# Scale and shift of the second adaLN branch: summed over the partitions by GpSimd instead of TensorE, with the conditioning loads moved forward

## The chip, the cores and the metric

One Trainium2 chip, one of its cores. The metric is the device time of one launch in microseconds (us). The kernel before took 1150.16 us, the median of three runs (1148.13 to 1151.42).

## The reference

One decoder block on x of 1024 tokens by 1024 channels, float32. A conditioning vector c gives six vectors of 1024 numbers: shift, scale and gate for a mixer and for an MLP. The mixer normalises x, projects it, runs a pooling and a state-space mixer, and projects back ("output projection", `w_out`). The MLP normalises again, applies scale_f and shift_f, and runs two large matrix products.

```
mod = silu(c) @ w_ada + b_ada                       # 1024 -> 6 * 1024
shift_m, scale_m, gate_m, shift_f, scale_f, gate_f = split(mod, 6)
u = rms_norm(h, g_mix) * (1 + scale_m) + shift_m
h = h + gate_m * (mixer(u) @ w_out)
u = rms_norm(h, g_mlp) * (1 + scale_f) + shift_f
h = h + gate_f * (square(relu(u @ w_up)) @ w_down)
out = rms_norm(h, g_final)
```

The change concerns how shift_f and scale_f (kinds 3 and 4 of the six) are computed.

## The kernel before

Tokens lie on the 128 partitions in eight tiles of 128 (`tok`). Each float32 product is made from three products of split halves (`hi` and `lo`): `mm3`, line 247, where nearly all TensorE work is. A weight tile is loaded by SyncE (SP) into `raw`, a ring of four buffers, copied to `hi` by ScalarE (ACT, L198), and the remainder `lo` is made by VectorE (DVE, L199).

The stages around the change, in the order of the program:

- **The z projection**, second half: eight steps of 24 matmuls (`z_tok`, one token tile a step). VectorE evacuates each step's PSUM bank (L908, L910), the last four steps also transpose two groups of 128 mixed channels each (`ymix`).
- **The output projection**, `gemm2(h)`, for the token halves h = 0 and 1, each in two column halves n = 0 and 1. A column half is 12 steps of 12 matmuls into four PSUM banks; at its end `out(i)` multiplies each bank by the gate (VectorE, L1000, into `tmp`, two buffers) and adds the product to `tok` (GpSimd, L1001, one of the sixteen on VectorE). In n = 1 of h = 0 each of the first eight steps also transposes for the other token half (L141), which needs a free PSUM bank.
- **Normalising for the MLP**, at the start of `gemm2(1)`: `norm_xn` takes a row scale from GpSimd (`rst`, L183) and makes `xn`; after ten more microseconds of planned time `u2_h0` transposes it (L1067) and applies `sc_f` and `sh_f`.

The conditioning work rides along. `ada_chunk(kind, q, dst)` covers 512 of the 1024 numbers of one kind: eight loads of 128x512 of `w_ada` through the same ring `raw` (L846), each multiplied by the activated c of its 128 rows and summed on VectorE into `acc` (L852 the first, L854 the other seven). `acc` then holds 128 partial sums for each number, one on each partition. For the gates (kinds 2 and 5) TensorE adds them up with a matrix of ones over split halves. For kinds 3 and 4 `fin` does it with four float32 matmuls with `acc` as weights and a column of ones (L879; eight records in the trace for each `fin`), so that the result arrives as columns, one number a partition; VectorE adds the bias (L882) and, for kind 4, multiplies by g_mlp (L884). `ada_tick(n)` issues n loads and does the sums of the loads before. A tick is called once for each step: 1 load in the first half of the z projection from its fifth step on, 3 in the second half, 1 in n = 0 and 2 in n = 1 of `gemm2(0)`, 1 in `gemm2(1)`. The chunks are taken in the order (2,0), (2,1), (3,0), (4,0), (3,1), (4,1), and (5,0), (5,1) later.

The order of instructions on each engine is fixed when the program is built, by the scheduler of the framework from planned times; `defer` and `step` only give it a planned clock. On the chip each engine then works through its own list in order, and an instruction that waits holds back all that stands behind it on that engine.

Of the kernel before, what the change touches and what calls it, by code (L numbers as in the profile page):

```python
# [2 lines left out]

# [5 lines left out]

# [8 lines left out]
P = 128  # L18
# [54 lines left out]
def tile_hybrid_block(  # L73
# [49 lines left out]
    def enter(stack, **kw):  # L123
        return stack.enter_context(tc.tile_pool(reuse_waits="tile", **kw))
# [99 lines left out]
    def defer(us, fn):  # L224
        later.append((clock["t"] + us, fn))
# [613 lines left out]
    def ada_chunk(kind, q, dst):  # L839
        acc = {}  # L840
        parts = []
        lo = (kind * 2 + q) * HW

        def load(k):
            raw = rawm.tile([P, UM], F32, name="raw", tag="raw", bufs=4)[:, :HW]
            sp.dma_start(out=raw, in_=wada_r[:, k, lo:lo + HW])  # L846
            return lambda: work(k, raw)

        def work(k, raw):
            if k == 0:  # L850
                acc[0] = accp.tile([P, HW], F32, name="acc", tag="acc", bufs=ACCB)
                dve.tensor_scalar(out=acc[0], in0=raw, scalar1=cact[:, 0:1], scalar2=None, op0=ALU.mult)  # L852
            else:
                dve.scalar_tensor_tensor(out=acc[0], in0=raw, scalar=cact[:, k:k + 1], in1=acc[0],  # L854
                                         op0=ALU.mult, op1=ALU.add)
            if k == KD - 1:
                if kind in (2, 5):
                    defer(FIN2 - SPL if q == 1 else FIN1 - SPL, split_acc)
                else:
                    defer(FIN1, fin)  # L860

        def split_acc():
            v = (fp if kind == 2 else actp).tile([P, 2, HW], F32R, name="ghl", tag="a")
            act.copy(v[:, 0, :], acc[0])
            dve.tensor_tensor(out=v[:, 1, :], in0=acc[0], in1=v[:, 0, :].bitcast(F32), op=ALU.subtract)
            parts.append(v)
            defer(SPL, fin)

        def fin():
            a = acc[0]  # L870
            ps = bank()
            if kind in (2, 5):
                for i in range(2):
                    pe.matmul(ps, lhsT=onesr, rhs=parts[0][:, i, :], start=i == 0, stop=i == 1)
                v = dst[:, q * HW:(q + 1) * HW]
                dve.tensor_tensor(out=v, in0=ps, in1=v, op=ALU.add)
                return
            for i in range(4):
                pe.matmul(ps[:, i:i + 1], lhsT=a[:, i * P:(i + 1) * P], rhs=ones[:, 0:1], start=True, stop=True)  # L879
            b = C_BADA + 8 * kind + 4 * q  # L880
            v = dst[:, 4 * q:4 * q + 4]
            dve.tensor_tensor(out=v, in0=ps[:, 0:4], in1=pc[:, b:b + 4], op=ALU.add)  # L882
            if kind == 4:
                dve.tensor_tensor(out=v, in0=v, in1=pc[:, C_GMLP + 4 * q:C_GMLP + 4 * q + 4], op=ALU.mult)  # L884

        for k in range(KD):
            ada_q.append(lambda k=k: load(k))

    def ada_tick(n):
        todo = list(ada_n)  # L890
        ada_n.clear()
        for _ in range(n):
            if ada_q:
                ada_n.append(ada_q.popleft()())
        for f in todo:
            f()
# [49 lines left out]
    for si in range(2):  # L946
        for t in range(NT):
            if si == 0 and t == ZC:
                while side:
                    side.popleft()()  # L950
                flush(True)
                mx.close()
                lt = ctx.enter_context(ExitStack())
                lp = enter(lt, name="late", bufs=1)
                fp = enter(lt, name="fslots", bufs=12)
                gm = lp.tile([P, D], F32, name="gm", tag="gm")
                gf = lp.tile([P, D], F32, name="gf")
                sp.dma_start(out=gm, in_=b_ada[:, 2 * D:3 * D].broadcast_to([P, D]))
                sp.dma_start(out=gf, in_=b_ada[:, 5 * D:6 * D].broadcast_to([P, D]))
                for q in range(2):  # L960
                    ada_chunk(2, q, gm)
                for q in range(2):
                    ada_chunk(3, q, sh_f)
                    ada_chunk(4, q, sc_f)
                for h in range(2):
                    for n in range(2):
                        for kk in list(range(4, 12)) + list(range(4)):
                            specs.append((1, HW, [(0, HW, wout_r[:, kk:kk + 1, n * HW:(n + 1) * HW])], None))
            if si == 0 and t >= ZC:
                zw += [z_weights(k) for k in range(2 * (t - ZC), 2 * (t - ZC) + 2)]  # L970
            z_tok(si, t, zw if si else ks)
            if (si, t) == (1, 3):
                prefetch(2)
            step(5.2 if si else 2.6, 1)
            ada_tick(3 if si else 1)
            if si == 0 and t == NT - 1:
                norm_y(0, list(range(8)))
            if si == 1 and t in (3, 7):
                norm_y(1, list(range(t - 3, t + 1)))
            if si == 1 and t >= 4:  # L980
                ym[0] += ymix(0, actp, (2 * (t - 4), 2 * (t - 4) + 1))
# [10 lines left out]
    def gemm2(h):  # L992
        for n in range(2):
# [3 lines left out]
            def out(i):  # L997
                t = 4 * h + i
                tmp = lp.tile([P, HW], F32, name="tmp", tag="tmp", bufs=2)
                dve.tensor_tensor(out=tmp, in0=pss[i], in1=gm[:, ns], op=ALU.mult)  # L1000
                (dve if h + n + i == 5 else pool).tensor_tensor(out=tok[:, t, ns], in0=tok[:, t, ns], in1=tmp,  # L1001
                                                                op=ALU.add)

            def mm(q, w, i):
# [158 lines left out]
    load_up(1)
# [474 lines left out]
```

## Time and profile before

| what | value |
|---|---|
| median of three runs | 1150.16 us (1148.13 to 1151.42) |
| the profiled execution's own time | 1152.16 us |
| its span in the trace | 1150.5 us |
| TensorE (PE) busy | 1138.3 us, 99% |
| VectorE (DVE) busy | 822.2 us, 71% |
| ScalarE (ACT) busy | 562.6 us, 49% |
| GpSimd (POOL) busy | 148.2 us, 13% |
| z projection, second half | about 333 to 380 us |
| `gemm2(0)`, n = 0 and n = 1 | about 381 to 415 us, 415 to 455 us |
| `gemm2(1)` | about 455 to 525 us |

All times of the trace are microseconds from the start of its span; 1.7 us of the execution's own time lie outside the span. A row of a timeline has the start, the length, the engine, the line, the operation, what it writes and reads, and in brackets how long its engine stood idle before it and what ended that. In a row of a group the three numbers after the colon are the shortest, the median and the longest duration in nanoseconds.

### The profile page before, as it was taken

How to read it: one execution, taken by the hardware profiler on the slowest of the kernel's cores; microseconds unless marked ns; L12 is line 12 of the kernel's file. 1: busy time of each engine (PE TensorE's matmuls, PEld its weight loads, DVE VectorE, ACT ScalarE, POOL GpSimd, SP SyncE). 2: the span in 40 equal slices, each digit the busy share in tenths (PEclk: the TensorE clock that was granted, in tenths of full speed). 3: DMA queues.
4: the chain of work that ended last, by engine and by line, in shares of the span. 5: the costliest groups of instructions: out<-in, count | busy, mean ns of one | idle time of the engine just before them, and what ended most of it. 6: DMA issues, size and time to landing. Idle time of an engine off the chain costs nothing.

```text
span 1150.5 us, 15234 instructions
## 1 busy us (share of the span) xinstructions
PE 1138.3 (99%) x5541; PEld 948.1 (82%) x5541; DVE 822.2 (71%) x1230; ACT 562.6 (49%) x985; POOL 148.2 (13%) x188
## 2 busy tenths in 40 slices
PE   9999999999999999999999999999999999999997
PEld 9889887877898888888788888888888888888886
DVE  4769989967878667666987666665458744586985
ACT  4477575544354424545774444444434344434373
POOL 3011335425400012022000000000100000000030
PEclk9999999999999999999999999999999999999999
DMA  9932432223256656863165434342599835775832
GB/s 280 254 114 64 131 92 83 93 86 115 74 183 188 226 191 229 257 198 114 36 238 192 174 134 168 143 160 88 211 382 345 308 94 162 254 238 196 279 116 90
DMA packets 123899, 200.72 MB, mean 174 GB/s; under 512 B 8464, under 2 KB 65584, under 8 KB 121776
## 3 DMA queue, kind: packets, MB, share of 16 engines
q1 hardware_dynamic: 122464, 196.24, 50.9%
q0 software_dynamic: 1120, 3.21, 0.9%
q8 instruction: 43, 0.70, 0.3%
q10 hardware_dynamic: 240, 0.30, 0.1%
q14 instruction: 32, 0.26, 0.1%
HBM read 159.81 MB, written 39.91 MB: 174 GB/s over the span
## 4 chain that ended last, share of the span: by engine, by line
PE 79%; DVE 7%; DMA 7%; ACT 2%; issue 2%; POOL 1%; POOLq 0%; SPq 0%; DVEq 0%; ACTq 0%
PE bank L247 70%; DMA raw<-in_w_ada_dram 4%; PE bank L746 2%; DVE acc L854 2%; DMA raw<-ypool_d 1%; DMA raw<-in_w_out_dram 1%; DVE lo L199 1%; PE bank L141 1%; PE bank L750 1%; PE bank L338 1%; PE bank L743 1%; PE bank L821 1%; POOL rst L183 1%; POOL tok L1001 0%; DVE wx L1179 0%
## 5 line engine op out<-in xcount | busy, mean ns | idle before, releaser
L247 PE MATMUL bank<-u,hi 128*128 128x512 f32 x560 | 182.6, 405 | 0.5 <-ACT u L390 0.4
L247 PE MATMUL bank<-dlo,dhi 128*128 128x512 f32 (+1 forms) x464 | 177.2, 382 | 0.0
L247 PE MATMUL bank<-dhi 128*128 128x512 f32 (+1 forms) x464 | 177.2, 382 | 0.0
L247 PE MATMUL bank<-dhi,dlo 128*128 128x512 f32 (+1 forms) x464 | 177.1, 382 | 0.0
L1457 ACT CAST dhi<-fr 128x1024 fp32r<-128x1024 f32 x56 | 58.9, 1052 | 142.8 <-PE bank L247 109.1
L247 PEld LDWEIGHTS bank<-u,hi 128*128 128x128 f32 x560 | 103.7, 189 | 26.6 <-issue 4.8
L1458 DVE TENSOR_TENSOR dlo<-fr,dhi 128x1024 fp32r<-128x1024 f32 x56 | 68.4, 1222 | 78.6 <-ACT dhi L1457 77.9
L247 PE MATMUL bank<-hi,ym 128*128 128x512 f32 x384 | 123.6, 395 | 0.0
L247 PE MATMUL bank<-u,lo 128*128 128x512 f32 x280 | 110.2, 393 | 0.0
L198 ACT CAST hi<-raw 128x512 fp32r<-128x512 f32 (+2 forms) x101 | 62.9, 634 | 80.2 <-DMA raw<-in_w_out_dram 41.6
L247 PEld LDWEIGHTS bank<-dlo,dhi 128*128 128x128 f32 x464 | 87.2, 188 | 17.0
L247 PEld LDWEIGHTS bank<-dhi,dlo 128*128 128x128 f32 x464 | 87.2, 188 | 17.0
L247 PEld LDWEIGHTS bank<-dhi 128*128 128x128 f32 x464 | 87.2, 188 | 16.8
L199 DVE TENSOR_TENSOR lo<-raw,hi 128x512 fp32r<-128x512 f32 (+2 forms) x101 | 75.1, 752 | 30.3 <-ACT hi L198 29.9
L247 PE MATMUL bank<-E,whl 128*128 128x512 f32 x384 | 92.7, 391 | 0.1
L247 PEld LDWEIGHTS bank<-E,whl 128*128 128x128 f32 x384 | 71.7, 188 | 16.6 <-DVE whl L1231 0.9
L247 PEld LDWEIGHTS bank<-hi,ym 128*128 128x128 f32 x384 | 72.1, 188 | 14.8 <-ACT hi L198 0.2
L183 POOL TENSOR_TENSOR rst<-ssq,mhalf 128x1 f32<-128x1 f32 (+2 forms) x27 | 26.5, 984 | 401.7 <-DVE ssq L182 368.2
L247 PE MATMUL bank<-u,whl 128*128 128x512 f32 x312 | 75.6, 389 | 0.0
L247 PE MATMUL bank<-lo,ym 128*128 128x512 f32 x192 | 74.9, 390 | 0.2 <-DVE lo L199 0.2
L247 PEld LDWEIGHTS bank<-u,whl 128*128 128x128 f32 x312 | 58.5, 188 | 12.5 <-DVE whl L1231 0.5
L1231 DVE TENSOR_TENSOR whl<-wraw,whl 128x512 fp32r<-128x512 f32 x58 | 39.9, 688 | 38.4 <-ACT whl L1226 38.3
(272 smaller groups left out, 2144.9 us busy)
## 6 DMA issues: line engine op xcount, KB each, us to landing
f_d<-tok SPq DMA_DIRECT2D x16, 1792.0 KB, 7.1
wr<-in_w_down_dram SPq DMA_DIRECT2D x56, 512.0 KB, 5.6
fr<-f_d SPq DMA_DIRECT2D x53, 512.0 KB, 4.8
raw<-in_w_ada_dram SPq DMA_DIRECT2D x64, 256.0 KB, 2.9
wraw<-in_w_up_dram SPq DMA_DIRECT2D x15, 1024.0 KB, 5.3
raw<-in_w_in_dram SPq DMA_DIRECT2D x48, 256.0 KB, 3.1
raw<-in_w_out_dram SPq DMA_DIRECT2D x48, 256.0 KB, 3.1
tok<-in_x_dram SPq DMA_DIRECT2D x16, 512.0 KB, 6.4
```

Of the source, the lines that this page charges most:

```text
L141: return pe.transpose(dst, src, ident)
L183: pool.tensor_tensor(out=rst[:, a:b], in0=m, in1=mhalf[:, :b - a], op=ALU.pow)
L198: act.copy(hi[:, :n], raw[:, :n])
L199: dve.tensor_tensor(out=lo[:, :n], in0=raw[:, :n], in1=hi[:, :n].bitcast(F32), op=ALU.subtract)
L247: pe.matmul(ps, lhsT=st_, rhs=mv, start=first and i == 0, stop=last and i == 2, skip_group_check=more)
L338: pe.matmul(warm_ps[:, 0:P], lhsT=ones, rhs=ones, start=True, stop=True)
L743: pe.matmul(po, lhsT=C[:, cs], rhs=states[g], start=True, stop=True)
L746: pe.matmul(py[:, hh * HD:(hh + 1) * HD], lhsT=Ms[hh // 4][:, (hh % 4) * P:(hh % 4 + 1) * P], rhs=xdt[:, hh * HD:(hh + 1) * HD], start=Tru ...
L854: dve.scalar_tensor_tensor(out=acc[0], in0=raw, scalar=cact[:, k:k + 1], in1=acc[0], op0=ALU.mult, op1=ALU.add)
L1231: dve.tensor_tensor(out=t_[:, 1], in0=src, in1=t_[:, 0].bitcast(F32), op=ALU.subtract)
L1457: act.copy(hi, src)
L1458: dve.tensor_tensor(out=lo, in0=src, in1=hi.bitcast(F32), op=ALU.subtract)
```

## The change

Five edits, all in one function.

1. For kinds 3 and 4 `fin` no longer exists. A new `across` lets GpSimd add `acc` up over the 128 partitions (`partition_all_reduce`, 128x512 in, the sum on every partition out), writes the sum's first row to a new DRAM buffer `mod_d` (a DMA of 2 KB on GpSimd's queue), and, after the second chunk of a kind, reads the 1024 numbers back as 128x8 columns straight into `sh_f` or `sc_f` (another DMA on GpSimd's queue, of 4-byte pieces). The four sums are kept in program order on GpSimd, so that they stand in one group.
2. `ada_cols_f`, called in `gemm2(1)`, adds the bias to both, and multiplies `sc_f` by g_mlp: three VectorE operations on 128x8.
3. The chunks of kinds 3 and 4 are now taken in the order (3,0), (3,1), (4,0), (4,1); the two chunks of a kind share a tile `macc`.
4. `ada_tick` takes 4 loads a step, not 3, in the second half of the z projection.
5. In `gemm2(0)` the eight adds to `tok` are done by VectorE (L1015) and no longer by GpSimd.

```
@@ ada_chunk
-                    defer(FIN1, fin)
+                    defer(15.5 if (kind, q) == (3, 0) else FIN1, across)
+        def across():
+            row = accp.tile([P, HW], F32, name="acc", tag="acc", bufs=ACCB)
+            tc.keep_in_program_order(pool.partition_all_reduce(row, acc[0], P, bass_isa.ReduceOp.add))
+            qs = slice(q * HW, (q + 1) * HW)
+            tc.keep_in_program_order(pool.dma_start(out=mod_d[kind - 3:kind - 2, qs], in_=row[0:1, :]))
+            if q == 1:
+                tc.keep_in_program_order(
+                    pool.dma_start(out=dst, in_=mod_d[kind - 3:kind - 2, :].rearrange("o (i p) -> p (o i)", p=P)))
...
-            for i in range(4):
-                pe.matmul(ps[:, i:i + 1], lhsT=a[:, i * P:(i + 1) * P], rhs=ones[:, 0:1], start=True, stop=True)
-            b = C_BADA + 8 * kind + 4 * q
-            v = dst[:, 4 * q:4 * q + 4]
-            dve.tensor_tensor(out=v, in0=ps[:, 0:4], in1=pc[:, b:b + 4], op=ALU.add)
-            if kind == 4:
-                dve.tensor_tensor(out=v, in0=v, in1=pc[:, C_GMLP + 4 * q:C_GMLP + 4 * q + 4], op=ALU.mult)
+    def ada_cols_f():
+        for kind, v in ((3, sh_f), (4, sc_f)):
+            b = C_BADA + 8 * kind
+            dve.tensor_tensor(out=v, in0=v, in1=pc[:, b:b + 8], op=ALU.add)
+        dve.tensor_tensor(out=sc_f, in0=sc_f, in1=pc[:, C_GMLP:C_GMLP + 8], op=ALU.mult)
@@ the z projection
-                for q in range(2):
-                    ada_chunk(3, q, sh_f)
-                    ada_chunk(4, q, sc_f)
+                for kind, dst in ((3, sh_f), (4, sc_f)):
+                    for q in range(2):
+                        ada_chunk(kind, q, dst)
-            ada_tick(3 if si else 1)
+            ada_tick(4 if si else 1)
@@ gemm2
-                (dve if h + n + i == 5 else pool).tensor_tensor(out=tok[:, t, ns], in0=tok[:, t, ns], in1=tmp,
+                (dve if h + n + i == 5 or h == 0 else pool).tensor_tensor(out=tok[:, t, ns], in0=tok[:, t, ns], in1=tmp,
@@ in gemm2(1)
+        if (n, q) == (0, 2):
+            ada_cols_f()
```

How the lists of the engines change. GpSimd, from the end of the z projection to `gemm2(1)`, before (`rst` are row scales of norms, the second 128x4 being that of the mixer's last four token tiles; `tok<-tok,tmp` are the adds of `out`):

```order
L183 TENSOR_TENSOR rst<-ssq,mhalf 128x8
L183 TENSOR_TENSOR rst<-ssq,mhalf 128x4 x2
L1001 TENSOR_TENSOR tok<-tok,tmp 128x512 x8
L183 TENSOR_TENSOR rst<-ssq,mhalf 128x1 x4
L1001 TENSOR_TENSOR tok<-tok,tmp 128x512 x5
```

The same place after, with the buffers' numbers (the `ISA` rows with operands are the sums over partitions, `macc_3823` holding kind 3 and `macc_4061` kind 4; the `ISA` without operands is the change of GpSimd's code library that the sums need):

```order
L184 TENSOR_TENSOR rst_129<-ssq_128,mhalf_130 128x4 x2
L869 ISA
L869 ISA acc_4084<-macc_3823 128x512
L871 DMA mod_d_69<-acc_4084 16x1x32
L869 ISA acc_4087<-macc_3823 128x512
L871 DMA mod_d_69<-acc_4087 16x1x32
L874 DMA sh_f_127<-mod_d_69 128x8x1
L869 ISA acc_4220<-macc_4061 128x512
L871 DMA mod_d_69<-acc_4220 16x1x32
L869 ISA acc_4418<-macc_4061 128x512
L871 DMA mod_d_69<-acc_4418 16x1x32
L874 DMA sc_f_126<-mod_d_69 128x8x1
```

The eight adds have gone from there, and the group of four sums and six DMAs stands right behind the last row scale of the mixer; behind it come a second change of the library and the row scales of `norm_xn`.

VectorE, in n = 0 of `gemm2(0)`, before (`acc` are the sums of a chunk, `lo` the remainders of the output projection's weights):

```order
L854 SCALAR_TENSOR_TENSOR acc<-raw,cact,acc 128x512
L199 TENSOR_TENSOR lo<-raw,hi 128x512
L854 SCALAR_TENSOR_TENSOR acc<-raw,cact,acc 128x512
L199 TENSOR_TENSOR lo<-raw,hi 128x512
L854 SCALAR_TENSOR_TENSOR acc<-raw,cact,acc 128x512
L882 TENSOR_TENSOR sc_f<-bank,pc 128x4
L884 TENSOR_TENSOR sc_f<-sc_f,pc 128x4
L199 TENSOR_TENSOR lo<-raw,hi 128x512
```

The same place after (`dsh` is a difference of two halves of `sh_f`, before at the end of n = 1's first steps):

```order
L200 TENSOR_TENSOR lo<-raw,hi 128x512
L859 SCALAR_TENSOR_TENSOR macc<-raw,cact,macc 128x512
L200 TENSOR_TENSOR lo<-raw,hi 128x512
L859 SCALAR_TENSOR_TENSOR macc<-raw,cact,macc 128x512
L898 TENSOR_TENSOR sh_f<-sh_f,pc 128x8
L1194 TENSOR_TENSOR dsh<-sh_f 128x4
L859 SCALAR_TENSOR_TENSOR macc<-raw,cact,macc 128x512
```

The add to `sh_f`, called in `gemm2(1)`, has been moved by the scheduler into n = 0 of `gemm2(0)`: behind the fifth of the last chunk's eight sums, after as many `lo` as stood ahead of `sc_f` before, and it waits for the DMA of `sh_f`.

VectorE, at the end of n = 0, before (`tmp<-bank,gm` empties the four banks of n = 0):

```order
L854 SCALAR_TENSOR_TENSOR acc<-raw,cact,acc 128x512
L199 TENSOR_TENSOR lo<-raw,hi 128x512
L852 TENSOR_SCALAR acc<-raw,cact 128x512
L854 SCALAR_TENSOR_TENSOR acc<-raw,cact,acc 128x512
L199 TENSOR_TENSOR lo<-raw,hi 128x512
L854 SCALAR_TENSOR_TENSOR acc<-raw,cact,acc 128x512 x2
L199 TENSOR_TENSOR lo<-raw,hi 128x512
L1000 TENSOR_TENSOR tmp<-bank,gm 128x512 x4
```

The same place after:

```order
L859 SCALAR_TENSOR_TENSOR macc<-raw,cact,macc 128x512
L200 TENSOR_TENSOR lo<-raw,hi 128x512
L859 SCALAR_TENSOR_TENSOR macc<-raw,cact,macc 128x512
L200 TENSOR_TENSOR lo<-raw,hi 128x512
L859 SCALAR_TENSOR_TENSOR macc<-raw,cact,macc 128x512
L200 TENSOR_TENSOR lo<-raw,hi 128x512 x2
L898 TENSOR_TENSOR sc_f<-sc_f,pc 128x8
L899 TENSOR_TENSOR sc_f<-sc_f,pc 128x8
L200 TENSOR_TENSOR lo<-raw,hi 128x512
L1014 TENSOR_TENSOR tmp<-bank,gm 128x512 x2
L1015 TENSOR_TENSOR tok<-tok,tmp 128x512 x2
L1014 TENSOR_TENSOR tmp<-bank,gm 128x512 x2
```

The add to `sc_f`, which waits for the DMA of `sc_f`, now stands two `lo` behind the last sum of the chunk that goes into it, and one `lo` ahead of the operations that empty the banks of n = 0. The adds to `tok` stand among these.

More of the change, by code (lines that the diff above doesn't have):

```diff
@@ L5 @@
 import concourse.tile as tile
-from concourse import mybir
+from concourse import bass_isa, mybir
 from concourse.masks import make_identity
@@ L133, in tile_hybrid_block @@
     ypool_d = dramp.tile([4, P, S], F32, name="ypool_d")
+    mod_d = dramp.tile([2, D], F32, name="mod_d")
     hres_d = [dramp.tile([P, D], F32, name=f"hres{t}") for t in range(NT)]
@@ L841, in ada_chunk @@
         parts = []
+        wide = kind in (3, 4)
         lo = (kind * 2 + q) * HW
@@ L850, in work @@
             if k == 0:
-                acc[0] = accp.tile([P, HW], F32, name="acc", tag="acc", bufs=ACCB)
+                if wide and q == 0:
+                    hold[kind] = (fp if kind == 3 else md).tile([P, 2, HW], F32, name="macc",
+                                                                tag="a" if kind == 3 else "macc")
+                acc[0] = hold[kind][:, q, :] if wide else accp.tile([P, HW], F32, name="acc", tag="acc", bufs=ACCB)
                 dve.tensor_scalar(out=acc[0], in0=raw, scalar1=cact[:, 0:1], scalar2=None, op0=ALU.mult)
@@ L869, in fin @@
         def fin():
-            a = acc[0]
             ps = bank()
[L872 to L877, printed above, removed]
-            for i in range(4):
-                pe.matmul(ps[:, i:i + 1], lhsT=a[:, i * P:(i + 1) * P], rhs=ones[:, 0:1], start=True, stop=True)
-            b = C_BADA + 8 * kind + 4 * q
-            v = dst[:, 4 * q:4 * q + 4]
-            dve.tensor_tensor(out=v, in0=ps[:, 0:4], in1=pc[:, b:b + 4], op=ALU.add)
-            if kind == 4:
-                dve.tensor_tensor(out=v, in0=v, in1=pc[:, C_GMLP + 4 * q:C_GMLP + 4 * q + 4], op=ALU.mult)
+            for i in range(2):
+                pe.matmul(ps, lhsT=onesr, rhs=parts[0][:, i, :], start=i == 0, stop=i == 1)
+            v = dst[:, q * HW:(q + 1) * HW]
+            dve.tensor_tensor(out=v, in0=ps, in1=v, op=ALU.add)
         for k in range(KD):
             ada_q.append(lambda k=k: load(k))
+    hold = {}
+    def ada_cols_f():
[3 more added lines that the diff above has]
+        dve.tensor_tensor(out=sc_f, in0=sc_f, in1=pc[:, C_GMLP:C_GMLP + 8], op=ALU.mult)
     def ada_tick(n):
@@ L955, in tile_hybrid_block @@
                 fp = enter(lt, name="fslots", bufs=12)
+                mds = ExitStack()
+                md = enter(mds, name="mods", bufs=1)
                 gm = lp.tile([P, D], F32, name="gm", tag="gm")
@@ L1160, in tile_hybrid_block @@
     am.close()
+    mds.close()
     wlst = ExitStack()
```

## The prediction

> **What bounds the kernel now.** I read the page's busy times first, then what TensorE waits for, then the stages around the change by windows (columns: busy time and instructions of TensorE, its weight loads, VectorE, ScalarE, GpSimd; granted clock; DMA share; GB/s).
>
> ```profile
> PE 1138.3 (99%) x5541; PEld 948.1 (82%) x5541; DVE 822.2 (71%) x1230; ACT 562.6 (49%) x985; POOL 148.2 (13%) x188
> ```
>
> ```profile
> PE bank L141 <- DVE tmp L1000: 0.6, 1, 0.6
> ```
>
> ```profile
> 0.00:50.00 50.00, 48.38 (x301) 43.56 (x302) 29.43 (x85) 21.08 (x34) 8.99 (x38) 0.97 0.94 260
> 341.00:380.00 39.00, 39.00 (x186) 32.44 (x185) 30.80 (x50) 21.93 (x44) 1.51 (x1) 1.00 0.61 190
> 396.00:414.00 18.00, 18.00 (x85) 15.02 (x84) 10.56 (x19) 4.61 (x8) 0.00 (x0) 1.00 0.69 228
> ```
>
> TensorE is the bound: busy for 99% of the span, and without a gap in the two stages that the change enters. So only two things count: TensorE work taken away, and any new wait of TensorE, which is added to the end in full. Its one wait here is the 0.6 us ahead of the first transposes of n = 1 (L141), for a PSUM bank that VectorE's L1000 empties. The timeline of TensorE shows that place and the work to be removed:
>
> ```profile
> 386.09 0.39 PE L247 MATMUL bank<-hi,ym 128*128 128x512 f32 x1
> 386.32 0.95 PE L879 MATMUL bank<-ones,acc 128*128 128x1 f32 x8
> 387.12 0.49 PE L247 MATMUL bank<-hi,ym 128*128 128x512 f32 x1
> 387.45 0.40 PE L247 MATMUL bank<-lo,ym 128*128 128x512 f32 x1
> 387.69 0.63 PE L247 MATMUL bank<-hi,ym 128*128 128x512 f32 x2
> ...
> 418.89 0.66 PE L141 MATMUL bank<-ident,tok 128*128 128x128 f32 x4 [0.58 <-DVE tmp L1000]
> ...
> 425.34 0.95 PE L879 MATMUL bank<-ones,acc 128*128 128x1 f32 x8
> 426.14 0.64 PE L141 MATMUL bank<-ident,tok 128*128 128x128 f32 x4
> ```
>
> **What is removed.** Matmuls start 0.23 us apart (386.09 to 386.32). Without the group of eight the three behind it would start at 386.32, 386.55 and 386.78; they start at 387.12, 387.45 and 387.69, so a group costs 0.91 us between matmuls. Ahead of transposes it costs 425.34 to 426.14, 0.80. The order has two of each kind: 2 x 0.91 + 2 x 0.80 = 3.4 us. Two lie ahead of 418.89, which without them and without the 0.58 us wait would be 418.89 - 1.82 - 0.58 = 416.5. The most that the change can gain is 3.4 + 0.6 = 4.0 us. VectorE's four small adds go too; they hold nobody.
>
> **What is added: a chain on GpSimd that VectorE waits for.** The order shows VectorE's adds to `sh_f` and `sc_f` inside n = 0 of `gemm2(0)`, not in `gemm2(1)` where they are called. VectorE works in order: behind `sc_f` stand the next `lo` and the operations that empty the four banks of n = 0, and behind the first of those TensorE's transposes of n = 1. So I date the chain by the rows of before:
>
> ```profile
> 389.26 0.17 DVE L182 TENSOR_SCALAR ssq<-ssq 128x4 f32<-128x4 f32 x1
> 404.09 0.75 DVE L854 SCALAR_TENSOR_TENSOR acc<-raw,cact,acc 128x512 f32<-128x512 f32 x1 [0.68 <-DMA raw<-in_w_ada_dram]
> 404.76 0.15 DVE L882 TENSOR_TENSOR sc_f<-bank,pc 128x4 f32<-128x4 f32 x1
> 408.68 0.75 DVE L854 SCALAR_TENSOR_TENSOR acc<-raw,cact,acc 128x512 f32<-128x512 f32 x1 [0.99 <-DMA raw<-in_w_ada_dram]
> 418.15 1.28 DVE L1000 TENSOR_TENSOR tmp<-bank,gm 128x512 f32<-128x512 f32 x2
> 423.17 2.57 DVE L854 SCALAR_TENSOR_TENSOR acc<-raw,cact,acc 128x512 f32<-128x512 f32 x2
> ```
>
> ```profile
> 0.31 0.10 POOL L1624 MEMSET const-float32-0.0<- 128x1 f32 x1 [0.31 <-issue]
> 16.00 0.55 POOL L483 DMA_DIRECT2D dsk<-in_d_skip_dram  x1
> 389.51 1.01 POOL L183 TENSOR_TENSOR rst<-ssq,mhalf 128x4 f32<-128x4 f32 x1 [25.26 <-DVE ssq L182]
> 418.91 5.49 POOL L1001 TENSOR_TENSOR tok<-tok,tmp 128x512 f32<-128x512 f32 x4 [28.39 <-DVE tmp L1000]
> 460.34 0.55 POOL L183 TENSOR_TENSOR rst<-ssq,mhalf 128x1 f32<-128x1 f32 x1
> ```
>
> ```profile
> raw<-in_w_ada_dram SPq DMA_DIRECT2D x64, 256.0 KB, 2.9
> cum_d<-dec SPq DMA_DIRECT2D x1, 64.0 KB, 2.0
> wp<-in_w_pool_dram SPq DMA_DIRECT2D x4, 64.0 KB, 1.9
> adaa<-in_conv_w_dram POOLq DMA_DIRECT2D x1, 24.0 KB, 6.2
> nea<-in_a_log_dram POOLq DMA_DIRECT2D x1, 8.0 KB, 5.0
> ```
>
> ```profile
> L1000 DVE TENSOR_TENSOR tmp<-bank,gm x16: 676/684/692, 418.2 to 529.2; 128x512 f32<-128x512 f32 x16
> L1001 POOL TENSOR_TENSOR tok<-tok,tmp x15: 1282/1296/1745, 418.9 to 525.5; 128x512 f32<-128x512 f32 x15
> L1001 DVE TENSOR_TENSOR tok<-tok,tmp x1: 689/689/689, 530.4 to 530.4; 128x512 f32<-128x512 f32 x1
> L183 POOL TENSOR_TENSOR rst<-ssq,mhalf x27: 546/552/3733, 6.0 to 1145.1; 128x1 f32<-128x1 f32 x24, 128x4 f32<-128x4 f32 x2, 128x8 f32<-128x8 f32 x1
> L854 DVE SCALAR_TENSOR_TENSOR acc<-raw,cact,acc x56: 739/751/1779, 325.3 to 487.8; 128x512 f32<-128x512 f32 x56
> ```
>
> Unknown costs, each by the nearest rows:
>
> - A sum over partitions. Not less than one GpSimd pass over 128x512, 1.30 us; halving 128 partitions takes seven passes, 7 x 1.30 = 9.1. The rows do not lean to either end, so I take the geometric middle, 3.4 us.
> - The change of the library. The program's own first instruction on GpSimd is of this kind and its first memset starts at 0.31, so it may cost nothing; the other end is the slowest small load on GpSimd's queue, 6.2. I take a plain 256 KB load, 2.9.
> - The issue of a DMA on GpSimd: 0.55 (the row at 16.00).
> - The 2 KB store: 2.0, as the store of `cum_d`.
> - The load of 1024 separate numbers: between 1.9 (`wp`) and 6.2. Nearest in queue and size is `nea`, 5.0; I take that, though it ran at a DMA share of 0.94 and this place has 0.69.
>
> GpSimd is free at 389.51 + 1.01 = 390.5; no edit moves that by a sum I could give, since the last scale hangs on the z projection's last step. Then `sh_f` lands at 390.5 + 2.9 + 2 x 3.4 (two sums) + 3 x 0.55 + 2.0 + 5.0 = 408.9. VectorE comes to its add when the fifth sum of the last chunk is done, 404.09 + 0.75 = 404.8, and waits 4.1 us. TensorE does not feel that wait yet: twelve `lo` are made by then, and the thirteenth is wanted only when n = 1 begins, about 414. The last sum of the chunk, 408.68 + 0.75 = 409.4, becomes 413.5. From it: 3.4 + 0.55 + 2.0 + 0.55 + 5.0 = 11.5, and `sc_f` lands at 425.0. VectorE then does the two adds (0.3), one `lo` (0.6) and the first `tmp` (0.7): 426.6. TensorE's transposes start there and not at 418.89: 7.7 us late. The two groups behind this place give 1.6 back. **Sum: 7.7 - 1.6 = 6.1 us slower.** TensorE has no slack behind this place in which to win it back. The profiled execution took 1152.16, so 1158.3; it is 2.0 over the median of 1150.16, against which I forecast 1156.3.
>
> The Trainium skill (GPSIMD Engine Reference, "Instruction dispatch") says that the first call to a freshly loaded kernel pays about 6 us, measured 5.95, which no profile instruction shows. By 5.95 instead of 2.9 every date from there is 3.05 later and the sum is +9.2 us; no trace here shows such a load, unless the 0.31 us at the start counts against it.
>
> By the ends, one at a time: a sum of 1.30 puts `sh_f` at 404.7, no wait, and `sc_f` at 409.4 + 9.4 = 418.8, in all 0 us; a sum of 9.1 gives 23 us slower. A free library gives +3.2, one of 6.2 gives +9.4. A load of 1.9 gives 0, one of 6.2 +8.5.
>
> **Edits with little weight.** Four loads a step: the eight accumulations moved forward add 8 x 0.75 = 6 us to VectorE's 30.8 of 39 us, so 36.8; it stays just under full, and TensorE waits for it there only by way of banks, so I cost it at 0. If that cover goes, VectorE is some us late at the end of the projection; I allow 2. On SP eight more loads go ahead of the output projection's weights:
>
> ```profile
> 341.26 17.63 SPq L846 DMA_DIRECT2D raw<-in_w_ada_dram  x15
> 460.93 0.75 DVE L1060 TENSOR_SCALAR xn<-tok,rst 128x1024 f32<-128x1024 f32 x1 [1.70 <-POOL rst L183]
> ```
>
> At 17.63 / 15 = 1.18 us each that is 9.4 us, for weights whose first two tiles are already there; 0 again. The eight adds cost VectorE 0.69 each in place of 1.30 on GpSimd. At the end of n = 0 they stand behind the bank operations that TensorE wants first, so they hide beside the next 12 matmuls, 2.7 us; uncovered, four of them are 2.8. Beside GpSimd's adds two accumulations took 2.57 us instead of 1.5, so a sum over partitions may slow VectorE too, by at most the 1 us seen there. The second change of library stands ahead of the row scale at 460.34, with over 30 us to spare; should it be paid at the first use only, `xn` at 460.93 waits for it, 2.9 us more at most.
>
> **Rivals.**
>
> *The group fits.* The point is the chain from the last accumulation: TensorE waits for nothing if `sc_f` lands 1.6 us before 416.5, so at 414.9, which leaves 414.9 - 409.4 = 5.5 us for a sum, two issues (1.1), a store and a load. With 2.0 and 1.9 for these, 0.5 us would be left for the sum; it needs a faster round trip through DRAM than any row shows, or accumulations that end earlier than before because the ring is less crowded. Then the change gives 4.0 us: 1146.2. For it speaks that GpSimd is idle from 390.5 to 418.9.
>
> *The sums go partition by partition.* If a sum is 127 small steps at the 0.55 us of a 128x1 operation, it takes 70 us. Then `sh_f` lands at 390.5 + 2.9 + 140 + 1.65 + 2.0 + 5.0 = 542, the third and fourth sums end at 677.6, `sc_f` lands at 685.7, and the time is 1150.16 + 268.4 - 1.6 = 1417.0. The Trainium skill (GPSIMD Engine Reference, "Cross-partition") has 247,699 ns for a reduction along the partition axis of 128x2048, so 62 us for a quarter of it, an estimate near this; the trace has no such operation, and this one may be another.
>
> *The second library is paid late.* With the wait at `xn` this is 6.1 + 2.9 = 9.0 us slower, 1159.2.
>
> **How the numbers follow.** The forecast's case, VectorE waiting for the group, gets 0.70. Its own range goes from 0 (a fast sum or a fast load) to 13.8 us (a sum of 5.7 and the rest as taken: 6.1 + 3 x 2.3 = 13.0, and a little over): 1150.2 to 1164.0. The rival that fits gets 0.20, the late library 0.06, the serial sum 0.04. About 0.3%, 3.45 us, is what a measurement of this kernel can tell from no change. Of the forecast's 0.70, 0.46 lies over it, since of six ends two are at 0 and one at +3.2, and 0.24 within. Of the fitting rival 0.16 is a gain over 0.3% (4.0 is barely that) and 0.04 within. Faster 0.16; within 0.24 + 0.04 = 0.28; slower 0.46 + 0.06 + 0.04 = 0.56. The range takes in the fitting rival's 1146.2 and ends at 1164.0; left out are the serial sum and the longest sums, some 0.12.
>
> **What the profile after would show.** Right: TensorE's group L879 gone; on VectorE, idle time ahead of the adds at L898, the longer one at `sc_f`, ended by a DMA on GpSimd's queue; on TensorE one gap of about 8 us ahead of the first transposes of n = 1, put down to the first bank operation; nothing else new. Each unknown can then be read: the start of the first sum against the last `rst`, the starts of the first two sums, the landing of the two column loads. Wrong: no idle time at L898, or idle time there but no gap on TensorE, or a gap that stands in the z projection.

## The result and the profile after

| | before | after |
|---|---|---|
| median of five runs | 1151.07 us (1148.13 to 1152.06) | 1165.70 us (1164.40 to 1168.64) |
| span of the profiled execution | 1150.5 us | 1163.0 us |
| TensorE waits for VectorE ahead of the first transposes of n = 1 | 0.6 us | 12.2 us |

The changed kernel takes 1.0128 of the time of before, 95% interval 1.0107 to 1.0149: 14.7 us more, with 12.3 to 17.2 by the ends of the interval. The forecast was 6.1 us more; its range ended at 1164.0.

The page's first line, and the rows of TensorE's busy tenths and granted clock; each digit is a slice of 29 us:

```profile
PE 1137.3 (98%) x5509; PEld 946.1 (81%) x5509; DVE 831.5 (71%) x1235; ACT 562.9 (48%) x985; POOL 154.0 (13%) x190
...
PE   9999999999999949999999999999999999999997
...
PEclk9999999999999979999999999999999999999999
```

TensorE does 32 matmuls less than before (5541) in a longer span. The loss stands in one slice, and there the granted clock falls too. What TensorE and VectorE wait for:

```profile
PE bank L142 <- DVE tmp L1014: 12.2, 1, 12.2
PE bank L248 <- DVE lo L200: 2.6, 2, 2.4
```

```profile
DVE sc_f L898 <- DMA sc_f<-mod_d: 6.3, 1, 6.3
DVE sh_f L898 <- DMA sh_f<-mod_d: 3.9, 1, 3.9
```

The stages by windows, as of before (busy time and instructions of TensorE, its weight loads, VectorE, ScalarE, GpSimd; granted clock; DMA share; GB/s):

```profile
341.00:380.00 39.00, 39.00 (x187) 32.48 (x186) 32.69 (x51) 20.80 (x41) 1.51 (x1) 1.00 0.66 206
396.00:414.00 18.00, 17.61 (x78) 14.10 (x76) 10.45 (x10) 4.34 (x7) 10.73 (x6) 1.00 0.61 194
414.00:440.00 26.00, 11.82 (x41) 9.43 (x42) 15.73 (x25) 4.99 (x8) 6.60 (x5) 0.67 0.33 96
```

The z projection is still full (39.00 of 39), with VectorE at 32.69 and not at the 36.8 that the forecast counted; TensorE is idle for 14.2 us of the last row. So the chain of the forecast is there: VectorE waits at both adds for GpSimd's loads, and TensorE has one long gap ahead of the transposes. The timelines date it. GpSimd first (start, duration, and in brackets the idle time ahead):

```profile
390.31 1.44 POOL L184 TENSOR_TENSOR rst<-ssq,mhalf 128x4 f32<-128x4 f32 x1 [25.44 <-DVE ssq L183]
399.57 3.25 POOL L869 PARTITION_ALL_REDUCE acc<-macc  x1 [7.83 <-issue]
...
403.88 3.19 POOL L869 PARTITION_ALL_REDUCE acc<-macc  x1
...
421.30 3.61 POOL L869 PARTITION_ALL_REDUCE acc<-macc  x1 [5.43 <-DVE macc L859]
...
471.23 0.60 POOL L184 TENSOR_TENSOR rst<-ssq,mhalf 128x1 f32<-128x1 f32 x1 [42.55 <-DVE ssq L183]
```

Then VectorE in the same stage:

```profile
399.97 2.38 DVE L200 TENSOR_TENSOR lo<-raw,hi 128x512 fp32r<-128x512 f32 x1 [1.29 <-ACT hi L199]
...
403.55 3.07 DVE L859 SCALAR_TENSOR_TENSOR macc<-raw,cact,macc 128x512 f32<-128x512 f32 x1
...
409.59 0.75 DVE L859 SCALAR_TENSOR_TENSOR macc<-raw,cact,macc 128x512 f32<-128x512 f32 x1 [1.11 <-DMA raw<-in_w_ada_dram]
414.29 0.17 DVE L898 TENSOR_TENSOR sh_f<-sh_f,pc 128x8 f32<-128x8 f32 x1 [3.95 <-DMA sh_f<-mod_d]
...
420.45 0.75 DVE L859 SCALAR_TENSOR_TENSOR macc<-raw,cact,macc 128x512 f32<-128x512 f32 x1 [3.27 <-DMA raw<-in_w_ada_dram]
421.12 3.33 DVE L200 TENSOR_TENSOR lo<-raw,hi 128x512 fp32r<-128x512 f32 x2
430.72 0.17 DVE L898 TENSOR_TENSOR sc_f<-sc_f,pc 128x8 f32<-128x8 f32 x1 [6.27 <-DMA sc_f<-mod_d]
```

Two things stand here that the forecast did not have. The idle time ahead of the first sum is 7.83 us, not 2.9. And one VectorE operation beside each of three sums lasts until about half a microsecond before that sum's end: 2.38 in place of 0.69, 3.07 in place of 0.74, and 3.33 in place of 1.28 for two. That is 1.7 + 2.3 + 2.1 = 6.1 us of VectorE's time. The usual lengths are in these rows, the first of before and the second of the changed kernel away from the sums:

```profile
400.37 0.69 DVE L199 TENSOR_TENSOR lo<-raw,hi 128x512 fp32r<-128x512 f32 x1
```

```profile
437.67 1.28 DVE L200 TENSOR_TENSOR lo<-raw,hi 128x512 fp32r<-128x512 f32 x2
```

TensorE behind both:

```profile
415.98 0.80 PE L248 MATMUL bank<-lo,ym 128*128 128x512 f32 x1 [2.37 <-DVE lo L200]
...
432.35 1.12 PE L142 MATMUL bank<-ident,tok 128*128 128x128 f32 x4 [12.20 <-DVE tmp L1014]
...
437.32 0.60 PE L142 MATMUL bank<-ident,tok 128*128 128x128 f32 x4
```

The transposes start at 432.35 instead of 418.89, 13.5 us late. The four of them took 0.66 us before and take 1.12 now, and the next four start 4.97 us later where 3.24 lay between them before: the lower clock behind the gap (0.67 in the row from 414 to 440 us) costs another 1.7 us.

### The profile page after: what moved, and what is told of

It is laid out like the page before. It is cut to its first block, busy times and chain, and to the rows that moved or that the text cites. A ratio compares the mean times of both kernels' runs of the same rounds, so it can differ in the third digit from the quotient of the medians.

```text
span 1163.0 us, 15181 instructions
## 1 busy us (share of the span) xinstructions
PE 1137.3 (98%) x5509; PEld 946.1 (81%) x5509; DVE 831.5 (71%) x1235; ACT 562.9 (48%) x985; POOL 154.0 (13%) x190
## 4 chain that ended last, share of the span: by engine, by line
PE 56%; DVE 4%; ACT 1%; issue 1%; DMA 1%; POOL 0%; POOLq 0%; ACTq 0%; DVEq 0%; SPq 0%
PE bank L248 55%; DVE whl L1248 1%; DVE wx L1196 1%; DMA wraw<-in_w_up_dram 0%; DVE tok L1199 0%; PE bank L142 0%; DVE tok L1196 0%; PE bank L1081 0%; POOL rst L184 0%; DMA sc_f<-mod_d 0%; ACT E L1106 0%; DVE E L1111 0%; DVE tmp L1014 0%; DVE lo L200 0%; POOL tok L1015 0%
## 5 line engine op out<-in xcount | busy, mean ns | idle before, releaser
L248 PE MATMUL bank<-u,hi 128*128 128x512 f32 x560 | 183.1, 406 | 0.5 <-ACT u L391 0.4
L248 PE MATMUL bank<-dlo,dhi 128*128 128x512 f32 (+1 forms) x464 | 177.2, 382 | 0.0
L248 PE MATMUL bank<-dhi 128*128 128x512 f32 (+1 forms) x464 | 177.2, 382 | 0.0
L248 PE MATMUL bank<-dhi,dlo 128*128 128x512 f32 (+1 forms) x464 | 177.1, 382 | 0.0
L248 PEld LDWEIGHTS bank<-u,hi 128*128 128x128 f32 x560 | 103.8, 189 | 26.8 <-issue 4.8
L248 PE MATMUL bank<-hi,ym 128*128 128x512 f32 x384 | 124.9, 399 | 0.0
L248 PE MATMUL bank<-u,lo 128*128 128x512 f32 x280 | 110.3, 394 | 0.0
L248 PEld LDWEIGHTS bank<-dhi 128*128 128x128 f32 x464 | 87.2, 188 | 17.2
L248 PEld LDWEIGHTS bank<-dlo,dhi 128*128 128x128 f32 x464 | 87.2, 188 | 16.9
L248 PEld LDWEIGHTS bank<-dhi,dlo 128*128 128x128 f32 x464 | 87.2, 188 | 16.8
L248 PE MATMUL bank<-E,whl 128*128 128x512 f32 x384 | 92.6, 391 | 0.1
L248 PEld LDWEIGHTS bank<-hi,ym 128*128 128x128 f32 x384 | 73.5, 192 | 15.2
L248 PEld LDWEIGHTS bank<-E,whl 128*128 128x128 f32 x384 | 71.6, 188 | 16.6 <-DVE whl L1248 0.9
L248 PE MATMUL bank<-lo,ym 128*128 128x512 f32 x192 | 76.1, 396 | 2.4 <-DVE lo L200 2.4
L248 PE MATMUL bank<-u,whl 128*128 128x512 f32 x312 | 75.5, 389 | 0.0
L248 PEld LDWEIGHTS bank<-u,whl 128*128 128x128 f32 x312 | 58.5, 188 | 12.6 <-DVE whl L1248 0.5
```

The costliest lines, as they stand in the source:

```text
L248: pe.matmul(ps, lhsT=st_, rhs=mv, start=first and i == 0, stop=last and i == 2, skip_group_check=more)
```

## The experiments

Theory A: VectorE's wait in order at the two adds is the loss. Theory B: GpSimd's sums hold VectorE's own operations. Theory C: the small edits (four loads a step, the order of the chunks, the eight adds on VectorE) cost it. Each ratio is against runs of before made beside the kernel; microseconds are worked out from it at 1151.5.

**adds_late**

```diff
-            dve.tensor_tensor(out=v, in0=v, in1=pc[:, b:b + 8], op=ALU.add)
+            tc.keep_in_program_order(dve.tensor_tensor(out=v, in0=v, in1=pc[:, b:b + 8], op=ALU.add))
```

> The changed kernel with one thing moved: VectorE's two adds to sh_f and sc_f, and what follows from them, stand in gemm2(1) where they are called and not in n = 0 of gemm2(0); the order of all other engines is the same. Theory A (VectorE waits in order for the two column loads, and that is the whole loss): both waits of TensorE in this stage, 2.4 us at L248 and 12.2 us at L142, are gone, and the time is that of before less up to 4.0 us, about 1147 to 1149. Theory B (GpSimd's sums slow VectorE's own operations beside them, and VectorE is late for that): the stretched rows (2.38, 3.07 and 3.33 us in place of 0.7, 0.7 and 1.4) are 6 us of delay and stay, TensorE still waits some 6 us at L142, about 1153. Theory C (the four loads a step or the moved adds): no change, about 1165.

The adds start at 466.3 us here. Measured: 1157.19 us, ratio 1.0042 (1.0024 to 1.0060), so 4.8 us over before and 9.9 under the changed kernel (single runs lie between 1152.08 and 1160.10). TensorE's wait ahead of the transposes in this kernel, and the row behind it:

```profile
424.47 1.12 PE L142 MATMUL bank<-ident,tok 128*128 128x128 f32 x4 [4.91 <-DVE tmp L1014]
429.82 0.60 PE L142 MATMUL bank<-ident,tok 128*128 128x128 f32 x4
```

The wait at the adds is the larger part, but a loss stays that it cannot explain: neither A nor B alone gives it.

**adds_late_short**

```diff
-            tc.keep_in_program_order(pool.partition_all_reduce(row, acc[0], P, bass_isa.ReduceOp.add))
+            tc.keep_in_program_order(pool.tensor_copy(out=row[0:1, :], in_=acc[0][0:1, :]))
```

> As the kernel before this one, and GpSimd's four sums are replaced by a copy of one row, which leaves out the sum over partitions: no library change, and hardly any GpSimd work beside VectorE. Theory A: the same time as with the sums, within 1 us, since nobody waits for the group in time. Theory B: VectorE's rows are 0.7 us each again and the time is up to 6 us below that of the kernel with the sums.

Measured: 1149.80 us, ratio 0.9979 (0.9963 to 0.9995), so 2.4 us under before and 7.2 under the kernel with the sums. VectorE at the same place, now beside a copy of 1x512:

```profile
399.37 0.75 DVE L859 SCALAR_TENSOR_TENSOR macc<-raw,cact,macc 128x512 f32<-128x512 f32 x1
400.11 1.02 DVE L200 TENSOR_TENSOR lo<-raw,hi 128x512 fp32r<-128x512 f32 x1
```

Theory B holds for this part.

**short**: the one line of the experiment above in the changed kernel, with the adds in n = 0 of `gemm2(0)`. The add to `sc_f` stands where it stood; the scheduler put the one to `sh_f` further ahead, behind the first of the last chunk's eight sums and not behind the fifth.

> The changed kernel with its adds where they stand, in n = 0 of gemm2(0), and GpSimd's four sums replaced by a copy of one row, which leaves out the sum over partitions: no library change and no long GpSimd operation. With the adds late this group gave 1149.8, and its load of sc_f was issued at 418.34, 4.7 us after the last accumulation. Theory A (the wait in order costs by itself, sums or not): sc_f lands about 422, VectorE's first tmp is 5 to 6 us later than the 416.65 of that run, and the time is 1155 to 1158. Theory B (the sums' hold on VectorE is all that counts): 1150.

Measured: 1159.75 us, ratio 1.0060 (1.0047 to 1.0074), so 6.9 us over before. The wait at the adds costs 6.9 + 2.4 = 9.3 us even when no long sum and no library change is there. VectorE at both adds, and TensorE behind the second:

```profile
402.23 0.17 DVE L898 TENSOR_TENSOR sh_f<-sh_f,pc 128x8 f32<-128x8 f32 x1 [4.23 <-DMA sh_f<-mod_d]
...
418.36 0.72 DVE L200 TENSOR_TENSOR lo<-raw,hi 128x512 fp32r<-128x512 f32 x1 [0.29 <-ACT hi L199]
424.59 0.17 DVE L898 TENSOR_TENSOR sc_f<-sc_f,pc 128x8 f32<-128x8 f32 x1 [5.51 <-DMA sc_f<-mod_d]
```

```profile
426.22 1.11 PE L142 MATMUL bank<-ident,tok 128*128 128x128 f32 x4 [9.25 <-DVE tmp L1014]
432.04 0.60 PE L142 MATMUL bank<-ident,tok 128*128 128x128 f32 x4
```

**tiny** and **adds_late_tiny**: the library change without the long sums, with the adds in both places.

```diff
-            tc.keep_in_program_order(pool.partition_all_reduce(row, acc[0], P, bass_isa.ReduceOp.add))
+            tc.keep_in_program_order(pool.tensor_copy(out=row[0:1, :], in_=acc[0][0:1, :]))
+            tc.keep_in_program_order(pool.partition_all_reduce(row[:, 0:8], acc[0][:, 0:8], P, bass_isa.ReduceOp.add))
```

> As the kernel before this one, and behind each copy stands a sum over partitions of 8 columns in place of 512; the sum over the rest is left out. The library change is back (7.8 us of idle GpSimd ahead of the first sum in the changed kernel), the long sums are not. If the library's time goes into the end in full, as the prediction's sum had it, this is 7 to 8 us slower than the kernel before; if VectorE is late at the last accumulation only by what it waits at sh_f, it is 0 to 4 us slower, as the chain from the last accumulation holds no library change.

> The changed kernel with its adds in gemm2(1) and the four sums over 8 columns in place of 512, behind a copy of one row; the sum over the rest is left out. The library change stays (7.7 us), the long sums go. If the long sums hold VectorE, TensorE's waits are those of the kernel with late adds and no sums, 0.2 and 1.9 us, and the time is 1149 to 1151. If the library change itself stops VectorE or its loads, it is up to 1157, that of the kernel with late adds and the whole sums.

Measured: 1160.70 us, ratio 1.0063 (1.0050 to 1.0076), and 1150.20 us, ratio 0.9974 (0.9962 to 0.9987). The library change is there at full length in both (the first row is of the second kernel). With the adds late it costs nothing (0.6 us less, within what the intervals leave open). With the adds in n = 0 the time is 0.4 us over `short`, but that is not the price of the library change alone: in `tiny` the add to `sh_f` stands behind the fifth sum again and waits 3.42 us (the second row, L899 in this kernel), in `short` it waits 4.23 us at its earlier place.

```profile
399.79 0.43 POOL L870 PARTITION_ALL_REDUCE acc<-macc  x1 [7.84 <-issue]
```

```profile
412.65 0.17 DVE L899 TENSOR_TENSOR sh_f<-sh_f,pc 128x8 f32<-128x8 f32 x1 [3.42 <-DMA sh_f<-mod_d]
```

So the six kernels make a table, in us against before:

| | sums of 512 columns | of 8 columns | a copy |
|---|---|---|---|
| adds in n = 0 of `gemm2(0)` | +14.7 | +7.3 | +6.9 |
| adds in `gemm2(1)` | +4.8 | -3.0 | -2.4 |

Down the columns, the wait in order is 9.9, 10.3 and 9.3 us (the last with the add to `sh_f` at its earlier place); along the rows, the long sums are 7.4 and 7.8 against the small ones. The two add up.

**edits_alone**

```diff
-            ada_tick(3 if si else 1)
+            ada_tick(4 if si else 1)
...
-                (dve if h + n + i == 5 else pool).tensor_tensor(out=tok[:, t, ns], in0=tok[:, t, ns], in1=tmp,
+                (dve if h + n + i == 5 or h == 0 else pool).tensor_tensor(out=tok[:, t, ns], in0=tok[:, t, ns], in1=tmp,
...
-                for q in range(2):
-                    ada_chunk(3, q, sh_f)
-                    ada_chunk(4, q, sc_f)
+                for kind, dst in ((3, sh_f), (4, sc_f)):
+                    for q in range(2):
+                        ada_chunk(kind, q, dst)
```

> The kernel before with the change's small edits alone: four conditioning loads a step, both chunks of the shift ahead of those of the scale, and the eight adds of gemm2(0) on VectorE; TensorE's groups stay. Theories A and B: no change, up to 2 us slower, 1151 to 1153. Theory C: most of the loss, 1160 to 1165.

Measured: 1150.68 us, ratio 0.9997 (0.9986 to 1.0009). Theory C falls.

**no_groups** and **ceiling**: before without TensorE's small matmuls, and the same with the edits above.

```diff
-            for i in range(4):
-                pe.matmul(ps[:, i:i + 1], lhsT=a[:, i * P:(i + 1) * P], rhs=ones[:, 0:1], start=True, stop=True)
...
-            dve.tensor_tensor(out=v, in0=ps[:, 0:4], in1=pc[:, b:b + 4], op=ALU.add)
+            dve.tensor_copy(out=v, in_=pc[:, b:b + 4])
```

> The kernel before without TensorE's four groups of small matmuls; scale and shift get only the bias, so the sum over partitions is left out. This is the most that the change could win. By the gaps between matmuls 3.4 us, 4.0 with the wait ahead of the transposes: 1147.1 to 1147.7. Rival: the groups filled time in which TensorE would wait for banks or weights, then under 1 us: 1150 to 1151.

> The kernel before with the small edits, without TensorE's groups and with nothing on GpSimd in their place; scale and shift get only the bias, so the sum over partitions is left out. It is what any placing of the sums could reach at best: the kernel with late adds and no sums gave 0.21% less than before (2.4 us). If its small copies and loads on GpSimd cost nothing, this gives the same, 1148.5 to 1149.5; if TensorE's 1.9 us wait ahead of the transposes and the lower clock behind it are theirs, up to 4.0 us less than before, 1147.

Measured: 1151.61 us, ratio 0.9999 (0.9985 to 1.0013), and 1149.47 us, ratio 0.9970 (0.9954 to 0.9986), 3.5 us under before. The first is a miss: 3.4 us were expected and the interval ends at 1.7. TensorE's row there shows a part of it, a wait of 1.8 us where before had 0.6, since VectorE does not empty the bank sooner because TensorE comes sooner:

```profile
417.55 0.66 PE L141 MATMUL bank<-ident,tok 128*128 128x128 f32 x4 [1.82 <-DVE tmp L998]
420.80 0.60 PE L141 MATMUL bank<-ident,tok 128*128 128x128 f32 x4
```

The ceiling has nearly the same wait (1.66) and gains more; why the edits help only beside it, the runs do not settle, and the intervals touch (0.9985 and 0.9986).

**sums_unused**: the groups back on TensorE, the whole group on GpSimd kept for a tile that nobody reads.

```diff
                     defer(15.5 if (kind, q) == (3, 0) else FIN1, across)
+                    defer(FIN1, small)
...
-                    pool.dma_start(out=dst, in_=mod_d[kind - 3:kind - 2, :].rearrange("o (i p) -> p (o i)", p=P)))
+                    pool.dma_start(out=spare[:, 8 * kind - 24:8 * kind - 16], in_=mod_d[kind - 3:kind - 2, :].rearrange("o (i p) -> p (o i)", p=P)))
```

> The changed kernel with TensorE's four groups of small matmuls back and used, and the whole group on GpSimd kept for a spare tile that nobody reads: no engine waits for the group. With the small edits alone the time was 1150.7. Theory B: VectorE's operations beside the sums are held again, up to 7.4 us (what the sums cost when the adds were late), 1155 to 1158. Theory A alone: 1151.

Measured: 1159.32 us, ratio 1.0054 (1.0034 to 1.0073): 6.2 us for work that nobody waits for. VectorE is held as before; these are its rows beside the third and the fourth sum:

```profile
412.33 3.00 DVE L200 TENSOR_TENSOR lo<-raw,hi 128x512 fp32r<-128x512 f32 x1
...
417.18 2.93 DVE L200 TENSOR_TENSOR lo<-raw,hi 128x512 fp32r<-128x512 f32 x2 [0.32 <-ACT hi L199]
```

The profiled execution is one of the three shorter of seven (1155.35 to 1157.09; the other four took 1159.32 to 1163.09). In it TensorE waits 2.24 us ahead of the transposes (0.58 before), and the next four come 4.71 us later where 3.2 is usual; the rest of the 6.2 us stands at no single place.

**sums_late**, **late_loaded** and **late_loaded_short**: can the sums stand where VectorE's delay is covered? In all three the adds stand in `gemm2(1)`, and GpSimd first copies a column of the tile that VectorE makes from the fourth bank of n = 0 into a new tile `gate`, so the group starts behind it; the second and third pay the library change early, by a sum of 8 columns, and the third has copies for the sums.

```diff
                 dve.tensor_tensor(out=tmp, in0=pss[i], in1=gm[:, ns], op=ALU.mult)
+                if (h, n, i) == (0, 0, 3):
+                    tc.keep_in_program_order(pool.tensor_copy(out=gate[:, 0:1], in_=tmp[:, 0:1]))
...
+            if (si, t) == (1, 7):
+                gate = lp.tile([P, 8], F32, name="gate", tag="gate")
+                tc.keep_in_program_order(pool.partition_all_reduce(gate, mhalf, P, bass_isa.ReduceOp.add))
```

> The changed kernel with its adds in gemm2(1) and with the whole group on GpSimd held back until n = 0 of gemm2(0) is done: GpSimd first copies one column of the tile that VectorE makes from the fourth bank. The sums then run beside n = 1, about 427 to 447, where the next weights are further ahead. Theory: the holds on VectorE are covered there, and the time is that of the kernel without sums and with late adds, 1149 to 1151. Rival: n = 1 has no more slack than n = 0, and each of four sums costs up to 2.5 us, 1153 to 1158; or the row scales at 460 wait for the library to change back, up to 8 us more.

> The changed kernel with its adds in gemm2(1), a sum of 8 columns that nobody reads right behind the last row scale of the projection (it pays the library change there), and the four sums held back until the fourth bank of n = 0 is emptied. The sums then run from about 419 to 437 and their stores end ahead of the 442 at which VectorE wants a buffer of theirs, which stopped it for 6.5 us in the kernel with the late group. Theory (VectorE is held by each sum, and only in n = 0 has TensorE no cover for it): no wait over 1 us in either half, no faster than the kernel without sums, 1148.5 to 1150.5. Rival 1: the holds count in n = 1 as well, two to four of 2.5 us, 1154 to 1158. Rival 2: the 4 us that the kernel with the late group lost behind 503, in matmuls 1% further apart, come from sums beside n = 1 and come again, 1153 to 1155.

> The kernel with the late group and the library paid early, its four sums replaced by a copy of one row, which leaves out the sum over partitions; the library change, the gate, the stores and the loads stay. That kernel gave 0.28% more than before with TensorE's waits all but gone; its profile has 87 to 88 matmuls per 20 us from 500 to 820 where the ceiling has 89. If the sums' work beside n = 1 brings the wider spacing, this has 89 again and 1149 to 1150. If the library change or the late loads bring it, it stays at 87 to 88 and 1154 to 1157.

Measured: 1159.99 us, ratio 1.0061 (1.0049 to 1.0074); 1157.41 us, ratio 1.0028 (1.0013 to 1.0044); 1153.68 us, ratio 1.0013 (1.0001 to 1.0025). In the first, a new wait in order came: VectorE's next chunk wants a buffer that a store of the sums still reads, 6.5 us, in this row:

```profile
442.11 1.25 DVE L857 TENSOR_SCALAR acc<-raw,cact 128x512 f32<-128x512 f32 x1 [6.51 <-DMA mod_d<-acc]
```

In the second TensorE waits 1.5 us at the transposes and at most 0.4 at any other place of the stage, as the theory had it, and yet the time is 3.2 us over before. Its matmuls stand further apart in the up projection, and so they do without the sums; the ceiling, `late_loaded` and `late_loaded_short` from 600 to 700 us:

```profile
600.00:700.00 100.00, 100.00 (x443) 82.79 (x441) 67.62 (x105) 42.71 (x77) 0.00 (x0) 1.00 0.43 163
```

```profile
600.00:700.00 100.00, 100.00 (x435) 81.42 (x434) 68.02 (x106) 43.41 (x78) 0.00 (x0) 1.00 0.45 169
```

```profile
600.00:700.00 100.00, 100.00 (x436) 81.39 (x435) 67.28 (x105) 43.85 (x80) 0.00 (x0) 1.00 0.44 166
```

443 matmuls in 100 us against 435 and 436, at a clock that the column gives as 1.00 in each. So the sums are not the reason (rival 2 of `late_loaded` falls). Nor are the library change and the late loads, the other causes that `late_loaded_short` was built to show: the wider spacing is there in the second half of the z projection already, some 25 us ahead of the first library change (from 300 to 320 us, ahead of that half, these kernels and before have 139 matmuls alike). One step of 24 matmuls in the ceiling, and the same step in `late_loaded_short`:

```profile
360.75 5.71 PE L247 MATMUL bank<-zw,u 128*128 128x512 f32 x24
```

```profile
363.70 5.84 PE L248 MATMUL bank<-zw,u 128*128 128x512 f32 x24
```

`sums_late` has 5.84 us for that step too, and 436 matmuls from 600 to 700 us. These three kernels share the tile `gate`, in a pool that is opened just ahead of the one that holds the weights of the z projection; `sums_unused`, with its new tile `spare` in another pool, has 5.71 us and 440 matmuls. So a new tile that moves the ones behind it in SBUF is the likely cause, but the traces give no addresses and no run has the tile alone: it is not shown.

It changes how these three times are read. The up projection (from the last matmul of `gemm2(1)` to the first of the down product) takes 311.4 us in the ceiling and 315.4 and 315.3 us in `late_loaded` and `late_loaded_short`. Without those 4 us, an estimate, `late_loaded` would be 0.8 us under before and not 3.2 over. Against `late_loaded_short`, which has the same tile, its four long sums cost 3.2 - 1.5 = 1.7 us, where they cost 7.4 to 7.8 beside n = 0; the two intervals overlap. No kernel that computes all of it beat before.

## Why the prediction was wrong

The direction, the place and the chain were right; the size was not. The step that failed is the term for what the sums do to VectorE itself: a sum over partitions may slow VectorE "by at most the 1 us seen there", says the prediction, and it enters the sum as nothing. The runs show 7.4 to 7.8 us for the four sums. The same order with sums of 8 columns (`tiny`) cost 7.3 us, near the 6.1 of the forecast; with the long sums it cost 14.7.

Why the row misled: the two accumulations that took 2.57 instead of 1.5 stood beside GpSimd adds of 1.30, and their 1 us was carried over to a sum that the prediction itself put at 3.4 us. The rows of after read as a hold: what VectorE has under way ends 0.45 to 0.47 us ahead of the sum's end in each of the three, so the price goes with the length of GpSimd's operation, 3.2 us. The Trainium skill (SBUF — State Buffer, "Who interferes with whom") states a rule of this kind: an operation of VectorE with two inputs in SBUF and one of GpSimd that reads SBUF lock each other out, and the one that issues second blocks fully. The trace agrees in the size (3.07 us in place of 0.74); it differs in who loses, since the `macc` of 403.55 began 0.33 us ahead of the sum of 403.88 by the profile, whose times on GpSimd are rough, and was the one stretched. The runs show the hold, not where in the chip the two meet. The prediction did not weigh that rule.

Term by term:

- *Wait in order, 7.7 us late.* Measured 9.9 and 10.3 against the same kernels with late adds (9.3 in `short`). That it came so near is in part luck: its inner dates were wrong in ways that cancel. The sums took 3.2 to 3.6 each where 3.4 was taken. The store and the load are these rows:

```profile
mod_d<-acc POOLq DMA_DIRECT2D x4, 2.0 KB, 2.9
sh_f<-mod_d POOLq DMA_DIRECT2D x1, 4.0 KB, 3.4
sc_f<-mod_d POOLq DMA_DIRECT2D x1, 4.0 KB, 2.9
```

  So 2.9 where 2.0 was taken, and 3.4 and 2.9 where 5.0 was. (`nea`, 8 KB, was not the nearest in size: `adaa<-in_g_mlp_dram`, 4.0 KB on the same queue, took 5.9 in before, farther still from what came.) From the last accumulation's end (421.2) to `sc_f`'s add (430.7) lie 9.5 us, 11.5 in the forecast.
- *Library change, 2.9 us.* It took 7.8. The sum had let its time pass into the end one for one. With late adds it was worth nothing; what it is worth with the adds in n = 0 no run shows alone. In the changed kernel it puts `sh_f` off, but VectorE, held by the sums, comes to that add at 410.3 and not at 404.8, so that it waits 3.95 us, near the 4.1 of the forecast by luck.
- *The last accumulation, 413.5.* It ended at 421.2. The add to `sh_f` came 5.4 us later than forecast (414.3, not 408.9), and the load of the eighth sum, which VectorE waits 3.27 us for (0.99 before), was issued at 415.95 only, when VectorE had freed one of the four buffers. The wait at `sh_f` adds little to it: in `adds_late`, which has no add there, the last accumulation ended at 420.0 too, behind three held operations (2.73, 3.07 and 3.32 us) and waits of 2.22 and 2.83 us for loads. Ring buffers behind a stalled engine were not in the sum.
- *"TensorE does not feel that wait yet".* It did, 2.37 us at L248; that changed nothing, since VectorE set the transposes.
- *Gain, 3.4 and at most 4.0.* The groups' removal by itself gave 0.1 (1.7 at most), with the edits (the ceiling) 3.5 (1.6 to 5.3). With GpSimd's copies and loads in place 2.4 to 3.0 are left.
- *Edits at nothing.* Right: -0.3 us (-1.6 to +1.0).
- *Clock.* It was left out, and took 1.7 us behind the long gap.
- *Rivals.* The group did not fit, even as copies (`short`). The sums do not go partition by partition: 3.2 to 3.6 us, not 70. The second library change was hidden: the row scale at 471.23 waits for VectorE's `ssq`.

## What to carry to other kernels

Ask of an engine beside VectorE not only when its result is due but for how long each of its operations reads SBUF: count one VectorE operation stretched to the end of each, even if nobody needs the result. Look in the order at where a scheduler has put the consumer of a slow chain: here two adds of 0.2 us, put ahead of the place where they are called, cost 9.9 us. Before a removal is priced at the work removed, see who is late next at the same place. And when a variant is slower with no wait to show for it, compare a stage that lies ahead of every edited instruction.

## What was not expected of the hardware

- A change of GpSimd's library showed as 7.65 to 8.32 us of idle GpSimd ahead of the first sum in seven kernels (7.83 in the changed one), and as 5.91 in `sums_late`. The Trainium skill (GPSIMD Engine Reference, "Instruction dispatch") has 5.95 for the first call to a fresh library; only the last of these agrees, and the measurement decides.
- After a wait of TensorE of 1.9 us or more at the transposes the granted clock fell (from 417 to 423 us it is 0.72 in `adds_late_short`, 1.00 in the ceiling), and the next four transposes came 4.7 to 5.8 us later where 3.2 is usual: a wait of 1.94 (`adds_late_short`) was followed by 4.83, of 4.91 by 5.35, of 9.25 by 5.82. Waits of 1.46, 1.66 and 1.82 us were followed by 3.25, 3.27 and 3.25. The row of `adds_late_short`:

```profile
417.39 0.66 PE L142 MATMUL bank<-ident,tok 128*128 128x128 f32 x4 [1.94 <-DVE tmp L1014]
422.22 0.60 PE L142 MATMUL bank<-ident,tok 128*128 128x128 f32 x4
```

  So in these profiles, one of each kernel, a wait from 1.9 us on cost 1.5 to 2.6 us more than itself.
- Matmuls 1.8% further apart (435 and 436 in 100 us against 443), at a granted clock of 1.00, in the three kernels with the tile `gate`, are told above; the cause stays open.
